# The first block's front of a hybrid conformer/RWKV-7 decoder block: adaLN columns, low parts and the seam to the first projections

## The chip, the cores and the metric

The kernel runs on one core of one Trainium2 chip. The metric is the device time of one execution in microseconds (us); lower is better. The engines are named as the profile names them: PE (TensorE, matmuls), PEld (its weight loads), DVE (VectorE), ACT (ScalarE), POOL (GpSimd) and SP (SyncE, which here issues the DMAs). The engines work side by side, each runs its own instructions in program order, and semaphores hold an instruction until its inputs are there and its output buffer is free. SBUF is the on-chip memory of 128 partitions; PSUM is the memory that PE writes to.

## The reference, cut to what matters

The reference computes one decoder block for a sequence of 2048 tokens and a width of 1024, in float32:

```
mod = silu(c) @ ada_w + ada_b;  shift, scale, gate = split(mod, 3)
h   = rmsnorm(x, norm_g) * (1 + scale) + shift
p   = h @ w_in                       # 73 tiles of 128 columns
...                                  # conv branch and RWKV-7 branch from p
out = (sigmoid(g_conv) * y_conv + sigmoid(g_rwkv) * y_rwkv) @ w_out
x   = rmsnorm(x + gate * out, final_g)
```

The conv branch is a gated causal depthwise convolution with a layer norm. The RWKV-7 branch shifts its inputs by one token (`z + mu * (prev - z)`), has low-rank parts for decay and learning rate (the "LORA" tile of p), and a delta-rule state per head. The change touches only the first lines: `mod` from c, the first h, and the first products with w_in.

## The kernel before, in words

Tokens are worked in four blocks of 512. Activations lie transposed, channels on the 128 partitions, so h of a block is eight tiles of 128 channels by 512 tokens (k = 0 to 7). A float32 product is made of three PE products with the faster type float32r: each operand is split into a high part (a rounding copy on ACT) and a low part (the difference, a subtraction on DVE or POOL), and `mm3k` adds high x high, high x low and low x high. A projection of one weight tile takes 8 x 3 = 24 matmuls of 128x512.

A planner in the kernel's own code orders the later work. `note` (line 116) keeps modelled times for each engine, buffer and DMA; work is written as generators (`Task`, line 215) that yield a function for the time at which they can go on; `poll` (line 223) advances those whose modelled time has come, lower rank first. So the order of the instructions on each engine is fixed when the program is built, and follows from the modelled times up to there. `ahead` (line 629) keeps up to three weight loads (`Load`, line 551) under way: DMA into `w_st`, ACT's copy to `w_hi`, the subtraction to `w_lo`, and stores of both parts for the later blocks. `project` (line 633) takes the next load and a PSUM tile `ps_main` (two buffers, tag "main").

The first block's h is made by `hprep0` (line 813), whose order is written out by hand:

- The row c is loaded to all 128 partitions (`srow`), silu is taken as c * (1 + tanh(c/2)), with the half put in later. Four x tiles of 128 tokens are loaded, the squares of the first two are summed on ACT and of the last two on DVE, and the reciprocal root goes into four scaled identity matrices `dg`.
- `columns(k)` makes two columns of `mod` (shift and scale of channel tile k): two DVE operations over 1024 elements multiply the loaded adaLN rows `ada_st` with `srow` and accumulate. Four such buffers exist; `columns(k)` starts the load of k + 4.
- `turned(k)` transposes and scales x on PE with `dg` into a PSUM tile `ps_x`; ACT adds the columns' scale and shift (`hf`), and `hsplit` (line 784) makes `h_hi` on ACT and `h_lo` on DVE.
- Four weight tiles, in the order LORA, K, R, V, are multiplied with h as h comes: `wsplit` (line 852) splits one, `products(k)` (line 900) catches up with all k before. Their results stay in PSUM as `ps_f`: LORA and K in the two "main" buffers, R and V in two others.
- At k = 4 the loads of the next two weights begin. After the last products both are split, and their further steps become tasks.

After `hprep0` the constants are made on DVE (among them `mu1`, line 1743, which is 1 - mu), and the four tiles are evicted: `lora_split` (line 1540) and `proj` go through `shifted` (line 951), which on ACT makes `t` from PSUM with `mu1`, then two single columns, and on DVE the shifted sum. The first `ps_main` product needs the bank of the LORA tile, and the second that of K.

The weight buffers have tags: "w" has six buffers, which `wr` (line 722) also hands out to loads; "KR" and "tk" have four each and "La" one. A tag's buffers go round in turn, and a new tile waits until the old one's readers are done.

Of the kernel before, what the change touches and what calls it, by code (L numbers as in the profile page):

```python
# [9 lines left out]
F32 = mybir.dt.float32  # L10
F32R = mybir.dt.float32r
# [7 lines left out]
P = 128  # L19
# [24 lines left out]
WB = 6  # L44
LDB = 8
SLACK = 2.0
LEND = 1
LATE_W = ((), (1, 1, 2, 2), (1, 1, 2, 2), (0, 0, 0, 0))
NWX, NRAW, NRAWX, NLD, LDQ, POOLW, PRE = 4, 4, 2, 4, 4.0, 0.0, ()
# [33 lines left out]
def hybrid_block(ctx: ExitStack, tc: tile.TileContext, x, x_t, vecs, convk, w2a2, final_g, ada, w_in, w_co, w_ro, w_o, crow, out,  # L83
# [467 lines left out]
    class Load:  # L551

        def __init__(self, src, task=True):
            self.src, self.here, self.stored, self.hl = src, False, False, None
            self.prior = loads[-2] if len(loads) > 1 else None
            if task:
                Task(self.steps(), 1)

        def steps(self):
            if len(self.src) == 3:  # L560
                yield when(lambda: all(l_.here or len(l_.src) == 3 for l_ in loads))
                yield both(wr.room(1), when(lambda: self.src in wk))
                while len(raws.all) < NRAW:
                    raws.all.extend(slices(wr.take("w_raw").bitcast(F32)))
                    raws.add(*raws.all[-2:])
                    yield wr.room(1)
                yield both(wr.room(1), raws.room())
                raw, t_ = raws.take(), wr.take("w_c")
                slot_ = wr.held.pop(key(t_))
                hi, lo = self.hl = slices(t_)  # L570
                wr.held[key(hi)] = slot_
                nc.sync.dma_start(raw, wk[self.src])
                back = wlow.get(self.src)
                if back is not None:
                    nc.sync.dma_start(lo.bitcast(F32), back.bitcast(F32))
                yield ok(raw)
                nc.scalar.copy(hi, raw)
                if back is None:
                    yield ok(hi)
                    yield some()  # L580
                    quick().tensor_tensor(out=lo, in0=raw, in1=hi.bitcast(F32), op=ALU.subtract)
                raws.give(raw)
                self.here = True
                if back is None and self.src in plan:
                    i_ = "_".join(str(k) for k in self.src)
                    wlow[self.src] = dp.tile([P, TB], F32R, name=f"wl_{i_}", tag=f"wl_{i_}")
                    yield ok(lo)
                    nc.sync.dma_start(wlow[self.src].bitcast(F32), lo.bitcast(F32))
                self.stored = True
                return  # L590
            name, n = self.src
            back = kept.get(self.src)
            if back is not None:
                yield wr.room(2)
                self.hl = wr.take("w_hi"), wr.take("w_lo")
                for t_, b_ in zip(self.hl, back):
                    nc.sync.dma_start(t_.bitcast(F32), b_.bitcast(F32))
                self.here = self.stored = True
                return
            if self.prior is not None:  # L600
                yield when(lambda: self.prior.hl is not None)
            yield wr.room(1)
            st = wr.take("w_st").bitcast(F32)
            nc.sync.dma_start(st, wsrc[name][n])
            yield both(ok(st), wr.room(2))
            hi, lo = self.hl = wr.take("w_hi"), wr.take("w_lo")
            nc.scalar.copy(hi, st)
            yield ok(hi)
            dve = max(now[0], vt["POOL"]) > max(now[0], vt["DVE"]) + W2
            (nc.vector if dve else nc.gpsimd).tensor_tensor(out=lo, in0=st, in1=hi.bitcast(F32), op=ALU.subtract)  # L610
            wr.give(st)
            self.here = True
            if name in KEPT:
                i = "_".join(str(k) for k in (n if isinstance(n, tuple) else (n,)))
                back = [dp.tile([P, KT, P], F32R, name=f"k{p_}_{name}{i}", tag=f"k{p_}_{name}{i}") for p_ in "hl"]
                kept[self.src] = back
                nc.sync.dma_start(back[0].bitcast(F32), hi.bitcast(F32))
                yield ok(lo)
                nc.sync.dma_start(back[1].bitcast(F32), lo.bitcast(F32))
            self.stored = True  # L620
# [40 lines left out]
            nc.sync.dma_start(xt[:, m, :], x[t0:t0 + P, :])  # L661
            xs.append(xt[:, m, :])

    late = ExitStack()
    pm = ctx.enter_context(tc.tile_pool(name="pm", bufs=2, space=PSUM))
    l3 = ctx.enter_context(tc.tile_pool(name="l3", bufs=3))
    c1 = late.enter_context(tc.tile_pool(name="c1", bufs=1))
# [5 lines left out]
    xp = ctx.enter_context(tc.tile_pool(name="xp", bufs=HXB, side="right"))  # L673
    hp = ctx.enter_context(tc.tile_pool(name="hp", bufs=1, side="right"))
    e2 = ctx.enter_context(tc.tile_pool(name="e2", bufs=2, side="right"))
    pa = ctx.enter_context(tc.tile_pool(name="pa", bufs=PAB, space=PSUM))

    ab = vc("ada_b")
    bones = c1.tile([P, P], F32R, name="bones")
# [101 lines left out]
            hx.give(xf)  # L781
        hx.give(row)

    def hsplit(h, k, src):
        hi = hp.tile([P, TB], F32R, name="h_hi", tag="h_hi", bufs=HB)
        lo = hp.tile([P, TB], F32R, name="h_lo", tag="h_lo", bufs=HB)
        with tc.high_priority(HP):
            nc.scalar.copy(hi, src)
            nc.vector.tensor_tensor(out=lo, in0=src, in1=hi.bitcast(F32), op=ALU.subtract)
        h[0].append(hi)  # L790
        h[1].append(lo)

# [18 lines left out]
    front = {}  # L811

    def hprep0():
        srow = l3.tile([P, D], F32, name="srow", tag="KR", bufs=KRB)
        stmp = l3.tile([P, D], F32, name="stmp", tag="KR", bufs=KRB)
        nc.sync.dma_start(srow, crow.unsqueeze(0).broadcast_to([P, D]))
        xs = []
        xload0(xs)
        xload0(xs)
        nc.sync.dma_start(v, vecs)  # L820
        nc.scalar.activation(stmp, srow, AF.Tanh, scale=0.5)
        nc.vector.scalar_tensor_tensor(out=srow, in0=stmp, scalar=1.0, in1=srow, op0=ALU.add, op1=ALU.mult)

        mod = lt.tile([P, 24], F32, name="mod", tag="rn")
        ada_ = []
# [15 lines left out]
        ada_load()  # L841
        wst_load(T_LORA, whl, tag="w", bufs=WB)
        wst_load(T_K, whl, tag="w", bufs=WB)
        ada_load()
        wst_load(T_R, l3, tag="tk", bufs=TKB)
        ada_load()
# [4 lines left out]

        def wsplit():
            i = len(wf_)
            if i < 2:
                hi, lo = [whl.tile([P, KT, P], F32R, name=n_, tag="w", bufs=WB) for n_ in ("w_hi", "w_lo")]
            else:
                hi = l3.tile([P, KT, P], F32R, name="w_f", tag="tk", bufs=TKB)
                lo = (l3.tile([P, KT, P], F32R, name="w_f", tag="tk", bufs=TKB) if i == 2 else
                      lt.tile([P, KT, P], F32R, name="w_f", tag="La", bufs=1))
            nc.scalar.copy(hi, wst[i])  # L860
            nc.vector.tensor_tensor(out=lo, in0=wst[i], in1=hi.bitcast(F32), op=ALU.subtract)
            wf_.append((hi, lo))
            front[tiles_[i]] = (pm, px)[i // 2].tile([P, TB], F32, name="ps_f", tag=("main", "xo")[i // 2])

# [6 lines left out]
        ss = e2.tile([P, 5, NTT], F32, name="ss0", tag="ss0", bufs=1)  # L871
        s2, ss, rs, rt = ss[:, 0:2, :], ss[:, 2, :], ss[:, 3, :], ss[:, 4, :]
        sq_ = [hx0("xsq0") for _ in range(2)]
        for tt in range(NTT // 2):
            for half in range(2):
                hs = slice(half * TB, half * TB + TB)
                nc.scalar.activation(sq_[0], xs[tt][:, hs], AF.Square, accum_out=s2[:, half, tt:tt + 1])
                xd = xs[tt + 2][:, hs]
                nc.vector.scalar_tensor_tensor(out=sq_[1], in0=xd, scalar=1.0, in1=xd, op0=ALU.mult, op1=ALU.mult,
                                               accum_out=s2[:, half, tt + 2:tt + 3])  # L880
        ab, gb = vc("ada_b"), mod[:, 16:24]
        nc.vector.tensor_tensor(out=ss, in0=s2[:, 0, :], in1=s2[:, 1, :], op=ALU.add)
        nc.vector.tensor_scalar(out=ss, in0=ss, scalar1=1.0 / D, scalar2=RMS_EPS, op0=ALU.mult, op1=ALU.add)
# [15 lines left out]

        def products(upto):  # L900
            for i, (w, ti) in enumerate(zip(wf_, tiles_)):
                if i < upto:
                    for kk in range(done_[i], upto):
                        mm3k(front[ti], w, h, kk)
                    done_[i] = upto

        def columns(k):
            for m in range(2):
                nc.vector.scalar_tensor_tensor(out=ada_[k][:, m, :], in0=ada_[k][:, m, :], scalar=0.5, in1=srow,
                                               op0=ALU.mult, op1=ALU.mult, accum_out=mod[:, k + 8 * m:k + 8 * m + 1])  # L910
            if k + 4 < KT:
                ada_load()
# [4 lines left out]
        for k in range(KT):  # L917
# [3 lines left out]
            nc.scalar.activation(shift_col[:, ks], mod[:, ks], AF.Identity, bias=ab[:, ks])  # L921
            nc.scalar.activation(g_col[:, ks], mod[:, gs], AF.Identity, scale=vc("norm_g", k), bias=gb[:, ks])
            if k + 4 == KT:
                for _ in range(2):
                    loads.append(Load(plan.pop(0), False))
                    next_.append(loads[-1].steps())
                    for _ in range(2):
                        next(next_[-1])
                wkeep(0)
                wkeep(1)  # L930
                nc.sync.dma_start(ck, convk)
# [4 lines left out]
            nc.scalar.activation(hf, flat(hp_[k]), AF.Identity, scale=g_col[:, ks], bias=shift_col[:, ks])  # L936
            if k:
                products(k)
            hsplit(h, k, hf)
            if k < 3:  # L940
                wsplit()
        products(KT)
        wkeep(2)
        wkeep(3)
        for steps in next_:
            next(steps)
            w = next(steps)
            Task(steps, 1).when = w
        return h

    def shifted(ps, ti, make):
        mi = ti - T_R
# [776 lines left out]
        yield from pair(G, q, box)  # L1729

    with tc.manual_schedule():
        h = hprep0()
        hlg = cst.tile([P, KT], F32, name="hlg")
        hlb = cst.tile([P, KT], F32, name="hlb")
        nc.vector.tensor_scalar(out=hlg, in0=vc("conv_ln_g"), scalar1=0.5, scalar2=None, op0=ALU.mult)
# [13 lines left out]
        hrk = dcol("hrk", "rwkv_r_k", 0.5, 0.0)  # L1749
        hgg = dcol("hgg", "rwkv_gn_g", 0.5, 0.0)  # L1750
        hgb = dcol("hgb", "rwkv_gn_b", 0.5, 0.0)
        nc.vector.tensor_scalar(out=ck, in0=ck, scalar1=0.5, scalar2=None, op0=ALU.mult)
        side.extend((Task(side_work(), 3), Task(last_norm(), 3)))
        for b in range(NB):
# [538 lines left out]
```

## Time and profile before

| | |
|---|---|
| median of 3 runs | 2684.56 us (2675.53 to 2688.15) |
| profiled execution | 2684.93 us |
| its span, first to last instruction | 2683.2 us |
| mean granted TensorE clock | 0.989 |
| PE busy | 2588.4 us (96%) |
| DVE, POOL, ACT busy | 2186.9, 1316.5, 1189.6 us |
| DMA moved | 712.11 MB, mean 265 GB/s |

A profile row gives the start in us from the first instruction, the duration, the engine, the line, the operation, and out<-in by the program's names; in brackets the idle time of the engine before it and what ended that. Nearly all rows name L194, the helper that records every operation, so tiles tell the rows apart: `ps_x` are the transpositions, `ps_f` the front products, `ps_main` the later projections, `ada_st` the column sums, `xsq` the squares, `mu` is mu1. Matmuls are pipelined, so the distance from start to start counts and not their duration. The granted clock is a share of full speed.

### The profile page before, as it was taken

How to read it: one execution, taken by the hardware profiler on the slowest of the kernel's cores; microseconds unless marked ns; L12 is line 12 of the kernel's file. 1: busy time of each engine (PE TensorE's matmuls, PEld its weight loads, DVE VectorE, ACT ScalarE, POOL GpSimd, SP SyncE). 2: the span in 40 equal slices, each digit the busy share in tenths (PEclk: the TensorE clock that was granted, in tenths of full speed). 3: DMA queues.
4: the chain of work that ended last, by engine and by line, in shares of the span. 5: the costliest groups of instructions: out<-in, count | busy, mean ns of one | idle time of the engine just before them, and what ended most of it. 6: DMA issues, size and time to landing. Idle time of an engine off the chain costs nothing. (4 is left out here: it accounts for less than half of the span.)

```text
span 2683.2 us, 50707 instructions
## 1 busy us (share of the span) xinstructions
PE 2588.4 (96%) x18324; PEld 2083.4 (78%) x18324; DVE 2186.9 (82%) x3663; ACT 1189.6 (44%) x2307; POOL 1316.5 (49%) x1818
## 2 busy tenths in 40 slices
PE   6999999999999999999999999999999998999997
PEld 5877888777877888788778877878887776778786
DVE  6786889788878896978698878888888689898687
ACT  5544444443434433434434333434444454456443
POOL 0576758462558373827583856483727484000000
PEclk9999999999999999999999999999999998999999
DMA  9788778787786688967877888686766778798984
GB/s 351 271 301 309 263 266 284 258 293 232 240 286 237 230 282 270 317 208 269 273 249 237 289 262 263 218 312 207 267 199 213 242 252 300 252 328 313 343 270 161
DMA packets 390835, 712.11 MB, mean 265 GB/s; under 512 B 137508, under 2 KB 141944, under 8 KB 390584
## 3 DMA queue, kind: packets, MB, share of 16 engines
q1 hardware_dynamic: 390584, 708.87, 77.7%
q8 instruction: 144, 2.36, 0.3%
q14 instruction: 107, 0.88, 0.1%
HBM read 494.34 MB, written 213.26 MB: 264 GB/s over the span
## 5 line engine op out<-in xcount | busy, mean ns | idle before, releaser
L194 PE MATMUL ps_main<-h_hi,w_hi 128*128 128x512 f32 x2304 | 923.3, 401 | 7.5 <-DVE lora L194 4.7
L194 PE MATMUL ps_main<-h_hi,w_lo 128*128 128x512 f32 x2304 | 924.8, 401 | 4.4 <-POOL w_lo L194 2.6
L194 PE MATMUL ps_main<-h_lo,w_hi 128*128 128x512 f32 x2304 | 923.0, 401 | 0.0
L194 DVE SCALAR_TENSOR_TENSOR acc<-u,ck,acc 128x512 f32<-128x512 f32 x928 | 698.9, 753 | 26.8
L194 PEld LDWEIGHTS ps_main<-h_hi,w_hi 128*128 128x128 f32 x2304 | 434.8, 189 | 105.9 <-issue 7.6
L194 PEld LDWEIGHTS ps_main<-h_hi,w_lo 128*128 128x128 f32 x2304 | 434.6, 189 | 101.4 <-issue 5.7
L194 PEld LDWEIGHTS ps_main<-h_lo,w_hi 128*128 128x128 f32 x2304 | 435.0, 189 | 93.0 <-issue 5.0
L194 PE MATMUL ps_main<-h_hi,w_c 128*128 128x512 f32 x896 | 291.2, 404 | 6.9 <-DVE mr L194 4.5
L194 POOL TENSOR_TENSOR itmp<-La,TT 128x126 f32<-128x126 f32 (+22 forms) x496 | 204.6, 412 | 46.4 <-issue 13.3
L194 POOL TENSOR_TENSOR TT<-TT,itmp 128x126 f32<-128x126 f32 (+22 forms) x496 | 205.8, 415 | 38.8
L194 ACT ACTIVATE th<-ps_main 128x512 f32<-128x512 f32 x160 | 95.6, 597 | 284.0 <-PE ps_main L194 267.0
L194 PEld LDWEIGHTS ps_main<-h_hi,w_c 128*128 128x128 f32 x896 | 171.6, 192 | 50.3 <-issue 3.9
L194 POOL TENSOR_TENSOR w_lo<-w_st,w_hi 128x1024 fp32r<-128x1024 f32 x55 | 133.4, 2426 | 142.6 <-ACT w_hi L194 131.0
L194 PE MATMUL ps_main<-h_lo,w_c 128*128 128x512 f32 x448 | 180.9, 404 | 13.7 <-DVE h_lo L194 13.6
L194 ACT COPY uv<-xo 64x256 f32<-64x256 f32 (+1 forms) x192 | 80.9, 438 | 210.3 <-PE xo L194 155.1
L194 DVE SCALAR_TENSOR_TENSOR S<-xo,pe,Se 64x64 f32<-64x64 f32 x512 | 123.2, 280 | 49.8 <-PE xo L194 38.5
L194 PE MATMUL ps_main<-w_c,h_hi 128*128 128x512 f32 x448 | 140.1, 393 | 0.0
L194 ACT CAST w_c<-w_raw 128x512 fp32r<-128x512 f32 x168 | 102.1, 619 | 72.0 <-DMA w_raw<-wk_o 27.4
L194 DVE TENSOR_TENSOR As<-aux,maskA 128x512 f32<-128x512 f32 x128 | 82.4, 686 | 47.5 <-PE aux L194 46.9
L194 PEld LDWEIGHTS ps_main<-h_lo,w_c 128*128 128x128 f32 x448 | 86.3, 193 | 35.3 <-DVE h_lo L194 16.0
L194 ACT ACTIVATE Se<-S,pe 128x128 f32<-128x128 f32 x256 | 88.6, 395 | 39.9 <-DVE S L194 38.7
L194 ACT ACTIVATE t<-ps_main,mu 128x512 f32<-128x512 f32 x96 | 65.9, 686 | 80.5 <-PE ps_main L194 80.0
(299 smaller groups left out, 4520.0 us busy)
## 6 DMA issues: line engine op xcount, KB each, us to landing
w_hi<-kh_in SPq DMA_DIRECT2D x219, 512.0 KB
w_lo<-kl_in SPq DMA_DIRECT2D x219, 512.0 KB
w_st<-w_in_t SPq DMA_DIRECT2D x73, 512.0 KB
kh_in<-w_hi SPq DMA_DIRECT2D x71, 512.0 KB
kl_in<-w_lo SPq DMA_DIRECT2D x71, 512.0 KB
lny<-y_d SPq DMA_DIRECT2D x80, 256.0 KB
w_raw<-wk_o SPq DMA_DIRECT2D x56, 256.0 KB
ada_st<-ada_t SPq DMA_DIRECT2D x16, 512.0 KB
```

Source lines behind the costliest of these rows:

```text
L194: r = f(*a, **k)
```

## The change

- silu(c) is computed on one partition (4 KB loaded instead of the row for 128 partitions). Two matmuls with a row of `ones` (which holds 1/1024) spread it into a new PSUM tile `ps_s` of two banks; the columns read it from there, and their factor becomes 0.5 x 1024. That PSUM room is given back before the pool `pa` opens in its place, which therefore opens after the front.
- All eight squares are summed on ACT.
- Low parts: those of weight tiles 0 and 2 stay on DVE (`WDV`), those of 1 and 3 go to POOL; those of h go to POOL, but for k = 7 (`HDV`).
- `products(k)` takes tile i from i <= k instead of i < k.
- The split of weight tile 0 goes into the tag "KR". A "w" buffer is set aside early for the first next weight (`loads[0].st`). At k = 4 both next loads begin as before.
- `hprep0` becomes a generator: it pauses after k = 6, the constants but for the scaling of `ck` are made then, and it goes on with k = 7. Before the last products the first next weight is split; behind them a third load is begun, and only then the parts of tiles 2 and 3 are stored.

```diff
     def hprep0():
-        srow = l3.tile([P, D], F32, name="srow", tag="KR", bufs=KRB)
-        stmp = l3.tile([P, D], F32, name="stmp", tag="KR", bufs=KRB)
-        nc.sync.dma_start(srow, crow.unsqueeze(0).broadcast_to([P, D]))
+        crow_ = lt.tile([P, D], F32, name="crow", tag="La", bufs=1)[0:1]
+        stmp = l3.tile([P, D], F32, name="stmp", tag="KR", bufs=KRB)[0:1]
+        nc.sync.dma_start(crow_, crow.unsqueeze(0))
...
-        nc.scalar.activation(stmp, srow, AF.Tanh, scale=0.5)
-        nc.vector.scalar_tensor_tensor(out=srow, in0=stmp, scalar=1.0, in1=srow, op0=ALU.add, op1=ALU.mult)
+        nc.scalar.activation(stmp, crow_, AF.Tanh, scale=0.5)
+        nc.vector.scalar_tensor_tensor(out=crow_, in0=stmp, scalar=1.0, in1=crow_, op0=ALU.add, op1=ALU.mult)
+        srow = p0.tile([P, 2, TB], F32, name="ps_s", tag="ps_s")
+        for half in range(2):
+            nc.tensor.matmul(srow[:, half], ones[0:1], crow_[:, half * TB:half * TB + TB], start=True, stop=True)
+        srow = flat(srow)
...
         wst_load(T_K, whl, tag="w", bufs=WB)
+        loads.append(Load(plan.pop(0), False))
+        loads[0].st = wr.take("w_st")
...
-            if i < 2:
+            if i == 0:
+                hi, lo = [l3.tile([P, KT, P], F32R, name="w_f", tag="KR", bufs=KRB) for _ in range(2)]
+            elif i == 1:
                 hi, lo = [whl.tile([P, KT, P], F32R, name=n_, tag="w", bufs=WB) for n_ in ("w_hi", "w_lo")]
...
-            nc.vector.tensor_tensor(out=lo, in0=wst[i], in1=hi.bitcast(F32), op=ALU.subtract)
+            (nc.vector if i in WDV else nc.gpsimd).tensor_tensor(out=lo, in0=wst[i], in1=hi.bitcast(F32), op=ALU.subtract)
...
-        for tt in range(NTT // 2):
+        for tt in range(NTT):
             for half in range(2):
                 hs = slice(half * TB, half * TB + TB)
-                nc.scalar.activation(sq_[0], xs[tt][:, hs], AF.Square, accum_out=s2[:, half, tt:tt + 1])
-                xd = xs[tt + 2][:, hs]
-                nc.vector.scalar_tensor_tensor(out=sq_[1], in0=xd, scalar=1.0, in1=xd, op0=ALU.mult, op1=ALU.mult,
-                                               accum_out=s2[:, half, tt + 2:tt + 3])
+                nc.scalar.activation(sq_[half], xs[tt][:, hs], AF.Square, accum_out=s2[:, half, tt:tt + 1])
...
-                if i < upto:
+                if i <= upto:
...
-                nc.vector.scalar_tensor_tensor(out=ada_[k][:, m, :], in0=ada_[k][:, m, :], scalar=0.5, in1=srow,
+                nc.vector.scalar_tensor_tensor(out=ada_[k][:, m, :], in0=ada_[k][:, m, :], scalar=0.5 * D, in1=srow,
...
             if k + 4 == KT:
-                for _ in range(2):
-                    loads.append(Load(plan.pop(0), False))
-                    next_.append(loads[-1].steps())
-                    for _ in range(2):
-                        next(next_[-1])
+                loads.append(Load(plan.pop(0), False))
+                loads[1].prior = None
+                for l_ in loads:
+                    next_.append(l_.steps())
+                    w_ = [next(next_[-1]) for _ in range(2)]
...
-            hsplit(h, k, hf)
+            hsplit(h, k, hf, None if k in HDV else nc.gpsimd)
             if k < 3:
                 wsplit()
+            if k + 2 == KT:
+                yield
+        next(next_[0])
+        first_ = next(next_[0])
         products(KT)
+        ahead()
+        poll()
         wkeep(2)
         wkeep(3)
-        for steps in next_:
-            next(steps)
-            w = next(steps)
+        for steps, w in zip(next_, (first_, w_[1])):
             Task(steps, 1).when = w
-        return h
+        yield h
...
-        h = hprep0()
+        start_ = hprep0()
+        next(start_)
...
         hgb = dcol("hgb", "rwkv_gn_b", 0.5, 0.0)
+        h = next(start_)
+        first.close()
+        pa = ctx.enter_context(tc.tile_pool(name="pa", bufs=PAB, space=PSUM))
         nc.vector.tensor_scalar(out=ck, in0=ck, scalar1=0.5, scalar2=None, op0=ALU.mult)
```

More of the change, by code (lines that the diff above doesn't have):

```diff
@@ L46 @@
 SLACK = 2.0
+WDV = (0, 2)
+HDV = (7,)
 LEND = 1
@@ L553, in __init__ @@
         def __init__(self, src, task=True):
-            self.src, self.here, self.stored, self.hl = src, False, False, None
+            self.src, self.here, self.stored, self.hl, self.st = src, False, False, None, None
             self.prior = loads[-2] if len(loads) > 1 else None
@@ L602, in steps @@
             yield wr.room(1)
-            st = wr.take("w_st").bitcast(F32)
+            st = (self.st or wr.take("w_st")).bitcast(F32)
             nc.sync.dma_start(st, wsrc[name][n])
@@ L662, in xload0 @@
             xs.append(xt[:, m, :])
-    late = ExitStack()
+    late, first = ExitStack(), ExitStack()
     pm = ctx.enter_context(tc.tile_pool(name="pm", bufs=2, space=PSUM))
@@ L675, in hybrid_block @@
     e2 = ctx.enter_context(tc.tile_pool(name="e2", bufs=2, side="right"))
-    pa = ctx.enter_context(tc.tile_pool(name="pa", bufs=PAB, space=PSUM))
+    p0 = first.enter_context(tc.tile_pool(name="p0", bufs=1, space=PSUM))
     ab = vc("ada_b")
@@ L782, in xnorm, with hsplit @@
         hx.give(row)
-    def hsplit(h, k, src):
+    def hsplit(h, k, src, eng=None):
         hi = hp.tile([P, TB], F32R, name="h_hi", tag="h_hi", bufs=HB)
@@ L788, in hsplit @@
             nc.scalar.copy(hi, src)
-            nc.vector.tensor_tensor(out=lo, in0=src, in1=hi.bitcast(F32), op=ALU.subtract)
+            (eng or nc.vector).tensor_tensor(out=lo, in0=src, in1=hi.bitcast(F32), op=ALU.subtract)
         h[0].append(hi)
```

## The prediction

> **What bounds the kernel now.** I read the page's totals first, then the span in stretches of 100 us, then what TensorE (PE) waited for, then the first 60 us instruction by instruction. Page:
>
> ```profile
> span 2683.2 us, 50707 instructions
> PE 2588.4 (96%) x18324; PEld 2083.4 (78%) x18324; DVE 2186.9 (82%) x3663; ACT 1189.6 (44%) x2307; POOL 1316.5 (49%) x1818
> ```
>
> Stretches (columns: length, busy time and count of PE, PEld, DVE, ACT, POOL, granted clock, DMA share, GB/s):
>
> ```profile
> 0.00:100.00 100.00, 77.14 (x365) 62.98 (x366) 73.35 (x142) 52.83 (x99) 25.91 (x26) 0.97 0.88 328
> 100.00:200.00 100.00, 96.58 (x468) 77.12 (x467) 77.16 (x98) 49.91 (x86) 67.68 (x85) 0.98 0.81 286
> 2200.00:2300.00 100.00, 87.61 (x402) 68.02 (x402) 88.68 (x133) 49.06 (x89) 44.20 (x29) 0.93 0.89 303
> 2300.00:2400.00 100.00, 93.35 (x393) 74.67 (x392) 89.09 (x144) 44.00 (x77) 0.00 (x0) 0.97 0.81 278
> ```
>
> PE is the bound. Its 95 us without work sit in the first 100 us (22.9) and about 2200 to 2400 (12.4 and 6.7). The change touches the first 60 us alone; time won there reaches the end only because PE is nearly full behind it. PE's waits over the span (total, times, longest):
>
> ```profile
> PE ps_main L194 <- DVE h_lo L194: 14.9, 6, 5.5
> PE ps_main L194 <- DVE lora L194: 4.7, 1, 4.7
> PE ps_f L194 <- DVE h_lo L194: 3.2, 2, 2.0
> ```
>
> The last two lie in the front. Its end, in order of time (start, duration, engine, what):
>
> ```profile
> 43.09 0.48 PE L194 MATMUL ps_f<-h_hi,w_hi 128*128 128x512 f32 x1
> 49.33 2.00 ACT L194 CAST w_hi<-w_st 128x1024 fp32r<-128x1024 f32 x2 [4.47 <-PE ps_f L194]
> 50.46 2.37 POOL L194 TENSOR_TENSOR w_lo<-w_st,w_hi 128x1024 fp32r<-128x1024 f32 x1 [48.61 <-ACT w_hi L194]
> 51.19 0.40 PE L194 MATMUL ps_f<-h_hi,w_f 128*128 128x512 f32 x1
> 51.36 2.56 DVE L194 TENSOR_TENSOR w_lo<-w_st,w_hi 128x1024 fp32r<-128x1024 f32 x1 [5.78 <-ACT w_hi L194]
> 53.98 0.17 DVE L194 TENSOR_SCALAR mu<-v 128x25 f32<-128x25 f32 x1
> 54.19 0.69 ACT L194 ACTIVATE t<-ps_f,mu 128x512 f32<-128x512 f32 x1 [2.86 <-DVE mu L194]
> 55.44 0.75 DVE L194 SCALAR_TENSOR_TENSOR lora<-ps_f,v,t 128x511 f32<-128x511 f32 x1 [0.52 <-ACT carry L194]
> 56.25 0.80 PE L194 MATMUL ps_main<-h_hi,w_hi 128*128 128x512 f32 x1 [4.66 <-DVE lora L194]
> 59.00 0.26 ACT L194 ACTIVATE carry<-ps_f,v 128x1 f32<-128x1 f32 x1
> 59.68 0.39 PE L194 MATMUL ps_main<-h_hi,w_lo 128*128 128x512 f32 x1
> ```
>
> PE's last front product starts at 51.19; the first of the next projection needs a PSUM bank that the LORA tile holds. That tile was complete at 49.3 (ACT's cast was released then), but its eviction needs mu1, which DVE makes only after the low part of the second next weight. That subtraction ran 2.56 us, because POOL did one at the same time, and mu1 came at 53.98. Then the restart is slow: 56.25 to 59.68 holds 8 starts, 0.43 us each, where 43.09 to 51.19 holds 35 at 0.231. So the seam costs 56.25 - 51.6 = 4.65 us of waiting and 3.43 - 8 x 0.231 = 1.58 us of half clock.
>
> The front before that:
>
> ```profile
> 6.57 0.63 ACT L194 ACTIVATE xsq<-x 128x512 f32<-128x512 f32 x1 [0.30 <-DMA x<-x_in]
> 8.07 0.63 ACT L194 ACTIVATE xsq<-x 128x512 f32<-128x512 f32 x1
> 9.15 0.69 DVE L194 SCALAR_TENSOR_TENSOR xsq<-x 128x512 f32<-128x512 f32 x1 [1.62 <-DMA x<-x_in]
> 11.97 0.08 DVE L194 DVE_READ_ACCUMULATOR xsq<-x 128x1 f32 x1
> 14.49 1.22 DVE L194 SCALAR_TENSOR_TENSOR ada_st<-ada_st,srow 128x1024 f32<-128x1024 f32 x1
> 16.84 1.23 DVE L194 TENSOR_TENSOR w_lo<-w_st,w_hi 128x1024 fp32r<-128x1024 f32 x1
> 16.91 0.38 ACT L194 ACTIVATE g_col<-mod,v 128x1 f32<-128x1 f32 x1
> 18.13 0.62 ACT L194 CAST h_hi<-hf 128x512 fp32r<-128x512 f32 x1
> 18.66 1.04 ACT L194 CAST w_hi<-w_st 128x1024 fp32r<-128x1024 f32 x1
> 39.90 1.22 DVE L194 SCALAR_TENSOR_TENSOR ada_st<-ada_st,srow 128x1024 f32<-128x1024 f32 x1
> 42.28 1.05 PE L194 MATMUL ps_x<-dg,x 128*128 128x128 f32 x8
> ```
>
> DVE runs 16 adaLN column sums (14.49 to 41.12) with the weight and h low parts between them. Stretches of it, and the DMA engines from 5 to 45 us:
>
> ```profile
> 20.00:25.00 5.00, 2.02 (x11) 1.38 (x11) 5.00 (x10) 3.57 (x7) 0.00 (x0) 1.00 1.03 410
> 25.00:30.00 5.00, 4.96 (x19) 4.13 (x20) 5.00 (x7) 3.96 (x7) 0.00 (x0) 0.66 1.03 410
> 5.00:45.00 40.00, 26.80 (x132) 22.76 (x133) 33.41 (x66) 24.94 (x49) 0.00 (x0) 0.96 1.03 411
> ```
>
> DVE is full, PE starves until about 28 us, then runs without a gap to 51.6: late feeding costs PE at the front's end. DMA is full as well, so a quicker DVE soon meets the loads.
>
> **The change part by part.** *Start.* The c row comes as 4 KB for one partition, not 512 KB for 128. ACT and DVE waited for x tiles one and three at 6.57 and 9.15: 1.29 us per 512 KB. All later loads land 1.29 us earlier. Tanh and the product with c take as long on one partition (1024 elements), and two spreading products follow on an idle PE before 14 us: no cost. All eight squares go to ACT: 1.50 us a tile (6.57 to 8.07), from 5.3 to 11.3, against 12.05 on DVE now. The chain behind them starts 0.75 us earlier: column 0 at 13.75, its h_hi at 17.4 to 18.0.
>
> *Columns.* DVE loses two weight low parts (1.14 each, 16.84 to the next start) and seven of h. Now the loads set its pace: twenty transfers of 512 KB follow the last x tile up to the last ada half; 10.45 + 0.2 + 20 x 1.29 = 36.5 now, 35.2 after. With 1.15 us of work behind it the last column ends at 36.4, not 41.1. h(7) is split by 36.4 + 1.9 (g_col start to h_hi end on ACT, 16.91 to 18.75) + 0.7 = 39.0; PE will want it at 44, so 5 us of slack covers DVE, DMA and the eleven small constant operations moved in front of the last step.
>
> *POOL.* The low parts that move cost more there (nanoseconds, least/median/most):
>
> ```profile
> L194 POOL TENSOR_TENSOR w_lo<-w_st,w_hi x55: 2343/2403/2843, 50.5 to 531.3; 128x1024 fp32r<-128x1024 f32 x55
> L194 POOL TENSOR_TENSOR h_lo<-cells,h_hi x15: 1263/1721/1748, 2166.1 to 2237.0; 128x512 fp32r<-128x512 f32 x15
> L194 DVE TENSOR_TENSOR h_lo<-hf,h_hi x40: 628/692/2395, 20.3 to 2147.3; 128x512 fp32r<-128x512 f32 x40
> ```
>
> The columns now read srow from PSUM. That such a DVE operation runs beside POOL unslowed is shown later in the trace, two in 1.29 us:
>
> ```profile
> 93.64 1.28 POOL L194 TENSOR_TENSOR s_lo<-rk,rh 128x512 fp32r<-128x512 f32 x1
> 93.89 1.29 DVE L194 TENSOR_TENSOR As<-aux,maskA 128x512 f32<-128x512 f32 x2 [1.01 <-PE aux L194]
> ```
>
> So I take 1.26 for h and 2.40 for weights; the bounds are 1.75 and 2.84. POOL: h_lo(0) 18.05 to 19.3, K's w_lo to 21.7, h_lo(1) to 23.0. PE starts K's products one k earlier than now, so its queue waits for K's low part (21.7) with the next transposition behind it; harmless, since h(2)'s column ends at 22.1 anyway (nine transfers behind x land at 21.0, and 1.15). From h_lo(1) on PE has work to the end: R's low part on DVE, held by POOL's port until 23.0, ends 24.1 where its products are due at 24.4; V's on POOL ends 27.9, due 28.7. Left are 90 products and four transpositions of 0.81 (42.28 to 43.09): 23.0 + 90 x 0.231 + 4 x 0.81 = 47.0. With POOL at its upper bound h_lo(1) ends at 24.4 and the front at 48.5; POOL's whole load, 7 x 1.75 + 2 x 2.84 = 17.9 us from 18, is still done before PE needs it.
>
> *Cold clock in the front.* Now the 0.66 at 25 to 30 costs PE at most 0.34 x 5 = 1.7 us. PE will again idle some 2.5 us between 18 and 23, less than now. I take half, 0.8 (bounds 0 and 1.7): the front ends at 47.8. The Trainium skill, TensorE: Matmul & The Clock Gate, section "What's actually happening", ties the half clock to an idle window of about 3.4 us; by it no pause here is long enough and the sum would be 0.8 less, but this trace fell to 0.66 behind pauses of at most 2.0 us (the wait for h_lo above), so the measurement decides.
>
> *Seam.* The first next weight gets slots that are free early, is split before the last products, and mu1 is ready. LORA's tile is complete nine products before the end, 45.7; from eviction to restart the trace has 54.19 to 56.25 = 2.06; PE restarts at 47.8 at the earliest, say 48.1, with 0.3 us of pause, too short for a cold clock by any row here. The second weight's split now stands behind LORA's eviction; projection two needs it at 48.1 + 24 x 0.231 = 53.6. If it queues behind all four evictions (54.19 to 59.26, 5.1 us), it ends at 45.7 + 5.1 + 1.04 + 2.4 = 54.2: at most 0.6 us. I take 0. SP holds the third weight's load ahead of four stores; no product waits for these.
>
> *Sum.* Restart 56.25 - 48.1 = 8.15 earlier, and 1.58 of half clock gone: 9.7 us. Bounds: all of POOL's and the clock's upper ends and 0.6 for the second weight give 9.7 - 1.5 - 0.9 - 0.6 = 6.7; the lower end of the clock gives 10.5. The profiled execution took 2684.93 (1.7 us around its span), the median of the runs is 2684.56: 2684.9 - 9.7 = 2675.
>
> **The rivals.** *The gain is not carried.* All later order is written from modelled times that shift here. If 2000 us of rearranged work give the 9.7 back, the time is 2684. Against it: PE at 96 to 100% in nearly all later stretches. For it: some 53 us of small waits (95 - 22.9 - 19) that a new order can move.
>
> *The change of stages gets shorter.* From 2200 to 2400 PE lacks 19 us, 8 of them in waits for h_lo, and runs at 0.93 and 0.97. If the new order halves the waits for h_lo and part of the slow clock with them, 8 us more go: 2667.
>
> *It gets longer, and the kernel slower.* Same place, other sign: half as much again of those 19 us (9.5) and 5 us of cold clock make 14.5, so 2690. It decides from 9.7 us on. The 5.5 us wait shows that one operation out of place there costs that much.
>
> *POOL binds the front.* Bounds above: 2678; it lies in the forecast's own range.
>
> **How the numbers follow.** Forecast 2675, own range 2671 to 2680: 0.57. Not carried, 2684: 0.15. Shorter change of stages, 2667: 0.18. Longer, 2690: 0.10. About 0.5% (13.4 us) is what a measurement of this kernel can tell from no change: faster than 2671 is nearly all of the 2667 case and a tail of the forecast, 0.22; over 2698 is the far part of the 2690 case, 0.06; the rest, 0.72, is within. The range 2665 to 2688 leaves out the ends of the 2667 and 2690 cases.
>
> **What would show it.** Right: h low parts on POOL at 1.3 us; the last column near 36.4; the last front product near 47; mu1 before 40; the first ps_main product near 48 with no wait for lora over 1 us and starts 0.23 apart; all later marks 9 to 10 us earlier. Wrong: DVE columns stretched beside POOL; a new PE wait for w_lo at 53; a cold clock after 48; or the front won and the stretch 2200 to 2400 changed by more than 5 us.

## The result, and the profile after

The changed kernel takes 2673.56 us in the median of 12 runs (2668.82 to 2679.79); 12 runs of the kernel before beside it take 2683.43 (2672.99 to 2694.58). The ratio is 0.9964 with a 95% interval of 0.9952 to 0.9977, so the kernel is 9.9 us faster, 0.36%; 9.7 us were forecast. That is a real gain and a small one, inside the half per cent that the prediction called "within".

The profiled execution of the changed kernel took 2679.79 us, the slowest of its 12, and so its span is only 5.3 us shorter than before's. Single executions of after lie up to 11 us apart here, those of before up to 22. The gain is therefore read from medians, and the place where it arises from the first 60 us of the traces. The page's totals:

```profile
span 2677.9 us, 50719 instructions
PE 2591.1 (97%) x18328; PEld 2082.4 (78%) x18328; DVE 2177.5 (81%) x3645; ACT 1191.8 (45%) x2315; POOL 1330.8 (50%) x1828
```

The same four stretches of 100 us as before, with the same columns:

```profile
0.00:100.00 100.00, 87.25 (x414) 69.23 (x415) 70.25 (x132) 61.17 (x120) 46.06 (x41) 1.00 0.93 349
100.00:200.00 100.00, 96.53 (x471) 77.20 (x471) 80.79 (x101) 48.06 (x80) 73.11 (x96) 1.00 0.84 297
2200.00:2300.00 100.00, 87.36 (x376) 67.58 (x375) 88.17 (x133) 48.27 (x86) 38.49 (x26) 0.93 0.88 300
2300.00:2400.00 100.00, 93.35 (x393) 74.83 (x393) 89.61 (x146) 44.71 (x80) 0.00 (x0) 0.97 0.83 283
```

Of these four only the first changed: PE is busy for 87.25 us of it instead of 77.14. The two stretches at the change of stages, of which two rivals expected 8 us less or 14.5 more, have the same PE time to 0.3 us and the same granted clock. PE's waits over the span (total, times, longest):

```profile
PE ps_main L196 <- DVE h_lo L196: 15.0, 6, 5.6
PE ps_main L196 <- POOL w_lo L196: 3.8, 4, 1.7
PE ps_f L196 <- POOL w_lo L196: 1.1, 1, 1.1
```

The waits for `lora` (4.7) and for the front's `h_lo` (3.2) are gone. The first row is the change of stages, as before. The front itself, rows picked from the timeline in order of start:

```profile
13.25 1.21 DVE L196 SCALAR_TENSOR_TENSOR ada_st<-ada_st,ps_s 128x1024 f32<-128x1024 f32 x1
...
18.83 2.37 POOL L196 TENSOR_TENSOR w_lo<-w_st,w_hi 128x1024 fp32r<-128x1024 f32 x1
18.92 0.50 PE L196 MATMUL ps_f<-h_lo,w_f 128*128 128x512 f32 x1 [0.48 <-POOL h_lo L196]
19.95 1.22 DVE L196 SCALAR_TENSOR_TENSOR ada_st<-ada_st,ps_s 128x1024 f32<-128x1024 f32 x1 [0.84 <-DMA ada_st<-ada_t]
21.16 1.28 POOL L196 TENSOR_TENSOR h_lo<-hf,h_hi 128x512 fp32r<-128x512 f32 x1
21.25 0.50 PE L196 MATMUL ps_f<-h_hi,w_lo 128*128 128x512 f32 x1 [1.14 <-POOL w_lo L196]
22.40 0.48 PE L196 MATMUL ps_f<-h_hi,w_f 128*128 128x512 f32 x1
35.69 1.22 DVE L196 SCALAR_TENSOR_TENSOR ada_st<-ada_st,ps_s 128x1024 f32<-128x1024 f32 x1
37.91 0.17 DVE L196 TENSOR_SCALAR mu<-v 128x25 f32<-128x25 f32 x1
41.30 2.41 POOL L196 TENSOR_TENSOR w_lo<-w_st,w_hi 128x1024 fp32r<-128x1024 f32 x1 [3.40 <-ACT w_hi L196]
44.90 0.69 ACT L196 ACTIVATE t<-ps_f,mu 128x512 f32<-128x512 f32 x1 [3.73 <-PE ps_f L196]
46.53 0.39 PE L196 MATMUL ps_f<-h_hi,w_f 128*128 128x512 f32 x1
47.04 0.51 PE L196 MATMUL ps_main<-h_hi,w_hi 128*128 128x512 f32 x1
47.39 0.40 PE L196 MATMUL ps_main<-h_lo,w_hi 128*128 128x512 f32 x1
```

A column that runs beside POOL (19.95) takes 1.22 us as the first one does. After 22.40 PE has no gap: the last front product starts at 46.53 and the first `ps_main` product 0.51 later. `mu1` is made at 37.91, seven microseconds ahead of the eviction that needs it (44.90). In stretches of 5 us the clock stays full where before had 0.66 (25 to 30):

```profile
20.00:25.00 5.00, 3.86 (x21) 3.27 (x21) 4.75 (x7) 4.54 (x8) 3.02 (x3) 1.00 1.03 410
25.00:30.00 5.00, 5.00 (x27) 4.25 (x26) 4.70 (x9) 3.55 (x8) 4.39 (x3) 1.00 1.03 410
```

One wait is new, and no step of the prediction had it: that for the low part of the third next weight.

```profile
53.49 0.41 ACT L196 CAST wl<-wf 128x256 fp32r<-128x256 f32 x1 [1.42 <-DMA wf<-w2a]
54.92 0.63 ACT L196 ACTIVATE xt<-xt 128x512 f32<-128x512 f32 x1 [0.53 <-DMA xt<-x_in]
56.16 1.03 ACT L196 CAST w_hi<-w_st 128x1024 fp32r<-128x1024 f32 x1
57.33 2.38 POOL L196 TENSOR_TENSOR w_lo<-w_st,w_hi 128x1024 fp32r<-128x1024 f32 x1 [2.36 <-ACT w_hi L196]
59.76 0.51 PE L196 MATMUL ps_main<-h_hi,w_lo 128*128 128x512 f32 x1 [0.98 <-POOL w_lo L196]
```

ACT takes that weight at 56.16, behind two operations that waited for DMAs. PE's products start at 58.39 and then only at 59.76, 1.14 us later than their pitch. So at 60 us the change stands at 9.21 (restart 56.25 to 47.04) + 1.58 (half clock gone) - 1.14 = 9.65 us, and the medians show 9.9 at the end. The 9.21 carries the spread of single executions: in another one of the same kernel (e11) the front starts 0.7 us earlier and the restart comes at 46.36.

A later mark shows how the lead goes on in this execution, the slowest of its 12. These are the DMA issues of `dA` in before and after (least, median and longest in ns, then the start of the first and the last in us):

```profile
L194 SPq DMA_DIRECT2D dA<-As x128: 302/449/1627, 137.4 to 2082.1; - x128
L196 SPq DMA_DIRECT2D dA<-As x128: 302/449/1779, 128.0 to 2077.7; - x128
```

The first is 9.4 us earlier, the last only 4.4. The prediction's sign that all later marks come 9 to 10 us earlier is thus seen up to 137 us; behind that it is borne out by the medians and not by this trace.

### The profile page after: what moved, and what is told of

Read it like the earlier page. It is cut to its first block, busy times and chain, and to the rows that moved or that the text cites. A ratio compares the mean times of both kernels' runs of the same rounds, so it can differ in the third digit from the quotient of the medians.

```text
span 2677.9 us, 50719 instructions
## 1 busy us (share of the span) xinstructions
PE 2591.1 (97%) x18328; PEld 2082.4 (78%) x18328; DVE 2177.5 (81%) x3645; ACT 1191.8 (45%) x2315; POOL 1330.8 (50%) x1828
## 5 line engine op out<-in xcount | busy, mean ns | idle before, releaser
L196 PE MATMUL ps_main<-h_lo,w_c 128*128 128x512 f32 x448 | 180.5, 403 | 13.8 <-DVE h_lo L196 13.7
```

Source lines behind the costliest of these rows:

```text
L196: r = f(*a, **k)
```

## The experiments

For each kernel the table gives two marks, counted from its own first transposition of x (the first `ps_x` start), because that start itself lies anywhere from 12.8 to 13.8 us in kernels with the same code up to there (13.81 in after, 13.10 in e11); of before there is one trace, with 15.05. Times with an interval are medians of 6 or 12 executions against the kernel before on the same chip; "1 run" is one execution.

| kernel | last front product | first `ps_main` | time, us | ratio to before |
|---|---|---|---|---|
| before | 36.14 | 41.20 | 2683.4 | |
| after | 32.72 | 33.23 | 2673.6 | 0.9964 (0.9952 to 0.9977) |
| e1, new front, old seam | 32.74 | 37.88 | 2680.0 | 0.9991 (0.9978 to 1.0004) |
| e2, old front, new seam | 35.71 | 36.14 | 2676.9 | 0.9974 (0.9964 to 0.9985) |
| e3, 80 more products | 32.73 | 51.27 | 2695.3 | 1.0050 (1.0033 to 1.0067) |
| e4, planner + 2 us | 32.74 | 33.25 | 2673.7 | 0.9962 (0.9945 to 0.9979) |
| e5, constants late | 32.72 | 33.23 | 2676.9, 1 run | |
| e6, h low parts on DVE | 36.14 | 36.57 | 2682.5, 1 run | |
| e7, products from i < k | 33.64 | 34.15 | 2676.8, 1 run | |
| e8, srow in SBUF | 37.34 | 37.85 | 2693.4, 1 run | |
| e9, later stores | 32.74 | 33.25 | 2677.4 | 0.9980 (0.9966 to 0.9995) |
| e10, planner + 6 us | 32.74 | 33.25 | 2682.8 | 1.0001 (0.9987 to 1.0014) |
| e11, after once more | 32.75 | 33.26 | 2674.9 | 0.9967 (0.9951 to 0.9982) |

**e1: the new front with the old seam.** Low parts, squares, silu and products as after; the next two weights are split behind the last products with the old buffers, and the constants come after all of it.

```diff
...
-        next(next_[0])
-        first_ = next(next_[0])
         products(KT)
-        ahead()
-        poll()
         wkeep(2)
         wkeep(3)
-        for steps, w in zip(next_, (first_, w_[1])):
+        for steps in next_:
+            next(steps)
+            w = next(steps)
             Task(steps, 1).when = w
...
```

> The changed kernel with the seam as before (weight tile 0 and the next weights in the old buffers, both next weights split behind the last products, constants made after that). Theory (the gain is made in the first 57 us and carried one for one): last front product near 46.5 as in the changed kernel, pause of about 4.7 us and a stretch at half clock as before, first ps_main product near 51.5, total about 6 us over the changed kernel, 2679 to 2680. Rival (the order of the later work gives the gain): the total need not follow the restart, and may be at 2674 or at 2684.

Its timeline, end of the front:

```profile
45.91 2.56 DVE L196 TENSOR_TENSOR w_lo<-w_st,w_hi 128x1024 fp32r<-128x1024 f32 x1 [5.76 <-ACT w_hi L196]
48.53 0.17 DVE L196 TENSOR_SCALAR mu<-v 128x25 f32<-128x25 f32 x1
50.87 0.80 PE L196 MATMUL ps_main<-h_hi,w_hi 128*128 128x512 f32 x1 [4.75 <-DVE lora L196]
51.47 0.63 PE L196 MATMUL ps_main<-h_lo,w_hi 128*128 128x512 f32 x1
```

The stall is back as it was: DVE's 2.56 us subtraction, `mu1` behind it, PE's wait of 4.75 us, and then products 0.43 us apart until 55.73. The front keeps its gain: from first transposition to last front product it takes 32.74 us (after 32.72, before 36.14). The time is 2680.0 against 2683.4, but its interval (0.9978 to 1.0004) includes no change, so these 3.4 us are not clear of noise.

**e2: the old front with the new seam.** All low parts on DVE, two x tiles' squares on DVE, products from i < k. Silu stays on one partition and in PSUM.

```diff
-WDV = (0, 2)
-HDV = (7,)
+WDV = (0, 1, 2, 3)
+HDV = tuple(range(8))
...
-                if i <= upto:
+                if i < upto:
```

> The changed kernel with all low parts of the front on DVE, products from i < k and the squares shared by ACT and DVE as before; silu stays in PSUM, the seam stays new. Theory: last front product at 50 to 51, pause under 0.5 us, no half clock behind it, first ps_main product near 51, total about 4 us over the changed kernel, 2677 to 2678. Rival: the total does not follow the restart.

The pause at the seam is 0.20 us beyond the pitch (49.09 to 49.52), and products follow 0.23 apart. The time is 6.5 us under before. With 3.4 from e1 that makes 9.9, the whole change, but that it fits so well is luck: both kernels keep the earlier start, which is thus counted twice. The marks leave the start out. By them the restart is 3.3 us earlier in e1, 5.1 in e2 and 8.0 in after, so front and seam add up to within 0.4 us; with the 1.58 of half clock, which e2 does not have, the seam is about two thirds. The trace held a surprise in the front, part of why the restart came at 49.52 where 51 was expected: first PE's timeline and then the stretches of 5 us:

```profile
23.36 0.50 PE L196 MATMUL ps_f<-h_lo,w_f 128*128 128x512 f32 x1 [2.01 <-DVE h_lo L196]
```

```profile
20.00:25.00 5.00, 2.99 (x17) 2.43 (x17) 5.00 (x8) 4.00 (x7) 0.00 (x0) 1.00 1.03 411
25.00:30.00 5.00, 4.21 (x23) 3.37 (x22) 5.00 (x9) 2.92 (x6) 0.00 (x0) 1.00 1.02 408
```

The same pause of 2.01 us that stood ahead of before's 0.66 left the clock at 1.00 here.

**e3: is time at the seam carried to the end?** Eighty more products between the front and the seam, past the planner, so that the order of all later work stays. They write the PSUM tile of silu(c), which nobody reads any more; their result is not used.

```diff
         products(KT)
+        for _ in range(80):
+            tc.nc.tensor.matmul(srow[:, 0:TB], wf_[0][0][:, 0, :], h[0][0], start=True, stop=True)
         ahead()
```

> The changed kernel with 80 extra matmuls of 128x512 on PE behind the last front products, written past the planner, so that every later instruction keeps its place; their result is not used. Theory: the restart comes 80 x 0.23 = 18.4 us later (near 65.4), the wait for the third weight (1.1 us) goes, and the total rises by 17 us, to about 2691: a us at the seam is a us at the end. Rival (the later stages absorb what happens at the start): a rise under 9 us.

The restart moved 18.0 us (33.23 to 51.27), the wait for the third weight is gone, and the median lies 21.7 above after's. So all of it is carried. The intervals reach 4.6 us to either side here and 3.4 in after, so the 3.7 us beyond what was put in are not clear of noise.

**e4 and e10: what the planner's order is worth.** The planner's modelled time is put forward by 2 and by 6 us behind the front. No work changes, only the order of what follows.

```diff
+        now[0] += 2.0        # 6.0 in e10
         side.extend((Task(side_work(), 3)
```

> The changed kernel with the planner's modelled PE time put 2.0 us ahead once, behind the front: the front is untouched, and the later order is another one. Theory: the total stays within 3 us of 2673.6. Rival (order alone is worth as much as the gain): it moves by 5 us or more.

> The changed kernel with the planner's modelled PE time put 6.0 us ahead once behind the front: a third order of the later work with the same front. Theory: within 4 us of the changed kernel, 2670 to 2678. Rival (order alone is worth as much as the gain): it moves by 5 us or more.

With 2 us the time did not move (2673.7). The wait for the third weight fell to 0.23 us there, because ACT took it at 54.68 ahead of the x tile's operations; a wait of 1.18 us for `lw` came behind it. With 6 us the front and the restart are after's, and yet the time is 2682.8, 8 us above e11 on the same chip. My theory expected 2670 to 2678 and fell. SP's one load of a weight between 27.3 and 57.3 us, ACT and PE behind the restart, and the clock in stretches of 20 us:

```profile
42.97 0.33 SPq L196 DMA_DIRECT2D w_st<-w_in_t  x1
47.10 1.05 ACT L196 CAST w_hi<-w_st 128x1024 fp32r<-128x1024 f32 x1 [1.74 <-DMA w_st<-w_in_t]
57.11 1.03 ACT L196 CAST w_hi<-w_st 128x1024 fp32r<-128x1024 f32 x1
58.20 0.79 PE L196 MATMUL ps_main<-h_hi,w_hi 128*128 128x512 f32 x1 [6.14 <-ACT w_hi L196]
58.79 0.63 PE L196 MATMUL ps_main<-h_lo,w_hi 128*128 128x512 f32 x1
60.68 0.80 PE L196 MATMUL ps_main<-h_hi,w_lo 128*128 128x512 f32 x1 [1.26 <-POOL w_lo L196]
```

```profile
40.00:60.00 20.00, 13.15 (x53) 9.63 (x52) 4.99 (x8) 11.33 (x26) 8.00 (x5) 0.90 0.96 353
60.00:80.00 20.00, 19.32 (x71) 15.34 (x72) 11.08 (x15) 9.51 (x17) 5.91 (x7) 0.84 0.58 220
```

PE waits after 24 products, so it wants the second weight, and gets it from the copy at 57.11. The copy at 47.10 waited for a load, and SP issued those of the first two weights from 26.38 on and then only the one at 42.97, which is the third weight's; so the third weight went ahead while the second lay ready. That reading is inferred from the counts and from SP's order, since rows do not name the weight. The sum is plain: 6.14 + 1.26 of waiting against e11's 1.34, and some 15 products at 0.43 instead of 0.23, make 9 us at 70 us. One copy out of place in an unchanged amount of work has cost by there nearly as much as the whole change won. That the loss reaches the end rests on the medians, whose intervals do not overlap: the two profiled executions end at 2679.9 and 2679.4, e11's being the slowest of its 12. Other effects of the new order further on are not excluded.

**e5: the constants' place.** They are made after the last products again, all else as after.

```diff
         next(start_)
+        h = next(start_)
         hlg =
...
-        h = next(start_)
         first.close()
```

> The changed kernel with the constants (mu1 among them) made behind the whole front instead of ahead of its last step. Theory (what was in mu1's way was the second next weight's low part on DVE, and that now comes later): DVE is idle from 40.9 on, the constants take 0.9 us there, and LORA's eviction starts unchanged when its products end, about 31.1 us behind the first transposition; restart unchanged within 0.2 us. Rival (the constants' place is what shortens the seam): restart a us or more later.

The restart is the same to 0.01 us. DVE's timeline:

```profile
40.22 0.17 DVE L196 TENSOR_SCALAR mu<-v 128x25 f32<-128x25 f32 x1
...
40.60 2.40 DVE L196 TENSOR_SCALAR ka<-v 128x8 f32<-128x8 f32 x1
```

`mu1` comes at 40.22, since no low part of a weight stands ahead of it on DVE any more. So this part of the change was not needed. The second row is a trap beside it: eight elements took 2.40 us, to 43.00, while POOL's `w_lo` ran from 40.52 to 42.97.

**e6: the low parts of h back on DVE.** The weight parts stay as after.

```diff
-HDV = (7,)
+HDV = tuple(range(8))
```

> The changed kernel with all of h's low parts on DVE. Theory: DVE's work for one k (2.3 for the columns and 0.6) is now longer than the loads need (2.58), each low part stands behind the next two columns, and the last column ends at 38 to 40; PE's backlog hides nearly all of it: restart 0 to 1 us later than in the changed kernel, from first transposition to restart 33.2 to 34.2 us. Rival (POOL for h is what feeds PE in time): 2 us or more later.

The restart is 3.34 us later, not 0 to 1, and the last front product stands at 36.14, as before: all of the front's gain is lost. Timeline of the place:

```profile
17.70 2.36 POOL L196 TENSOR_TENSOR w_lo<-w_st,w_hi 128x1024 fp32r<-128x1024 f32 x1 [15.85 <-ACT w_hi L196]
18.19 2.42 DVE L196 TENSOR_TENSOR h_lo<-hf,h_hi 128x512 fp32r<-128x512 f32 x1
20.66 0.51 PE L196 MATMUL ps_f<-h_lo,w_f 128*128 128x512 f32 x1 [1.98 <-DVE h_lo L196]
```

DVE's subtraction of two SBUF tiles is held until POOL's ends and takes 2.42 us instead of 0.69, PE waits 1.98, and behind that the clock falls, in the stretches of 5 us:

```profile
20.00:25.00 5.00, 4.34 (x16) 3.86 (x17) 5.00 (x8) 3.41 (x7) 0.06 (x1) 0.67 1.02 407
```

So POOL is not only relief for DVE's load: it is what keeps h's low parts out of the turn-taking with the weight's.

**e7: products from i < k.**

```diff
-                if i <= upto:
+                if i < upto:
```

> The changed kernel with products from tiles i < k as before. Theory: three products fewer are done before h's second tile is split, so three more stand in the gapless part: restart 0.7 us later, from first transposition to restart 33.9 us. Rival (the earlier start of K only makes PE wait for K's low part): restart unchanged or earlier.

The restart is 0.92 us later. That is what the one word is worth.

**e8: silu(c) copied to SBUF.** The columns read it there and no longer in PSUM.

```diff
-        srow = flat(srow)
+        srow_ = l3.tile([P, D], F32, name="srow_", tag="BK", bufs=BKB)
+        nc.scalar.copy(srow_, flat(srow))
+        srow = srow_
```

> The changed kernel with the spread silu row copied from PSUM to SBUF (one ACT copy of about 1 us near 9 us) and the columns reading it there. Theory (DVE with two SBUF inputs and POOL hold each other up): columns that meet a POOL operation take up to 3.6 us instead of 1.2, or POOL's operations up to 2.4 and 3.6 us instead of 1.3 and 2.4, the last column ends at 40 or later, and the restart comes 1 to 5 us later. Rival (where the row lies does not matter): column and POOL durations and restart unchanged.

Timeline of DVE and POOL where they meet:

```profile
21.80 1.50 POOL L196 TENSOR_TENSOR h_lo<-hf,h_hi 128x512 fp32r<-128x512 f32 x1 [19.94 <-ACT h_hi L196]
22.09 2.28 DVE L196 SCALAR_TENSOR_TENSOR ada_st<-ada_st,srow__457 128x1024 f32<-128x1024 f32 x1
23.25 3.33 POOL L196 TENSOR_TENSOR w_lo<-w_st,w_hi 128x1024 fp32r<-128x1024 f32 x1
24.30 3.37 DVE L196 SCALAR_TENSOR_TENSOR ada_st<-ada_st,srow__457 128x1024 f32<-128x1024 f32 x1
26.55 2.25 POOL L196 TENSOR_TENSOR h_lo<-hf,h_hi 128x512 fp32r<-128x512 f32 x1
```

The two engines now take turns. The column at 24.30 is long because it waits until POOL's `w_lo` ends at 26.58 and then needs its 1.1 us; POOL's next subtraction in turn waits for it. From its first transposition the restart is 4.6 us later than after's. (That first transposition is itself 4.2 us late: the copy waits on ACT for PE's spreading products, with the squares behind it.) The one run of 2693.4 lies 19.9 us above after's median; the restart, 8.8 us later in all (47.04 to 55.86), accounts for less than half of that, and the rest is open.

**e9: the stores behind the seam put off.** The stores of the split parts of tiles 2 and 3 become tasks 12 and 24 us later, to let ACT's inputs through earlier.

```diff
-        wkeep(2)
-        wkeep(3)
+        def keep_later():
+            for i in (2, 3):
+                yield after(12.0)
+                wkeep(i)
+
+        Task(keep_later(), 1)
```

> The changed kernel with the four stores of the split R and V tiles put off by 12 and 24 us of planner time, so that the loads behind them on SP's queue (low-rank weights, the next x) are issued earlier. Theory (the third weight's cast on ACT stands behind operations that wait for these loads): the wait of PE for the third weight's low part (1.1 us at 59.8) goes, at most 1 us of the total, which the timing cannot tell from nothing: 2671 to 2675. Rival (the third weight is late for its own load or slots): the wait stays.

The wait for the third weight is 0.58 us instead of 1.34 in e11: shorter, but not gone as the theory expected. The time is 2677.4 against 2674.9, and the intervals overlap, so no gain is seen.

**e11: the changed kernel again**, on the chip of e9 and e10.

> The changed kernel itself, on the chip of the two runs beside it, as their base. All theories: 2673 to 2676, and the marks of its front as in its first profile.

It took 2674.9, and its front's marks are after's.

## Why the prediction was right, point by point

**Start.** The first column was to move from 14.49 to 13.75, and it came at 13.25. That is a late one: in the nine other traces with the same start (all but e2 and e8) it comes at 12.24 to 12.55. This step was mis-sized, by 0.5 to 1.5 us: ACT's squares began at 4.78 (4.63 to 4.93 in the others), while 1.29 before 6.57 would be 5.28. No run takes the start away alone, and there is one trace of before, so its worth is not known better than that.

**Columns.** The last one ends at 36.91; 36.4 was forecast. The loads do set the pace: the columns at 19.95 and others now wait for `ada_st`.

**POOL.** The lower prices held (1.28 for h, 2.37 to 2.41 for weights), and `h_lo(1)` was ready at 22.44 instead of 23.0. The bet that a column which reads PSUM is not slowed by POOL rested on one pair of rows; e8 shows what it was worth, 4.6 us. The Trainium skill, SBUF — State Buffer, section "Who interferes with whom", states this rule: a DVE instruction with at most one SBUF input, outside the faster two-port modes, does not contend with GpSimd, and one with two SBUF inputs does. After (1.22) and e8 (2.28 and 3.37) agree with it.

**Cold clock in the front.** I took half of 1.7 us as left, and there was none. PE's pauses were 0.48 and 1.14 us, where 2.5 in all were forecast. This step was mis-sized by 0.8; it is most of why PE restarted at 47.04 and not at 48.1, and the earlier start is the rest. By the window of about 3.4 us that the Trainium skill, TensorE: Matmul & The Clock Gate, section "What's actually happening", gives, there was to be none, and after agrees; e6 does not, with 0.67 around a pause of 1.98. Nor does PE starve until about 28 us in before, as I wrote: its last pause in the front ends at 25.05, and from there to 28.40 products run 0.43 apart.

**Seam.** A pause of 0.3 was forecast, and the start-to-start distance of 0.51 leaves that over the pitch of 0.231. No half clock follows. The cause that I gave, `mu1` behind DVE's low part of the second weight, is what e1 brings back. But I listed three things together: an early split, free buffers and early constants. e5 shows that the constants' place is worth nothing once the low part has left DVE. The early split and the free buffers were not taken apart.

**What the prediction missed.** "I take 0" was right for the second weight, whose low part was ready at 50.66 for 52.7. It did not go one weight further: the third is split behind ACT operations that wait for DMAs, and costs 1.14 us. I followed SP's order only as far as the stores, and not to the loads behind them that ACT's queue waits for. So the sum of 9.7 came out this close by luck: a restart 1.06 us better than forecast paid for a wait of 1.14 that the forecast lacked.

**The rivals.** *Not carried* fell: e3's later restart came out in full at the end, and the medians of the change agree with the front's sum. *POOL binds* fell by its rows. *The change of stages shorter* or *longer* fell in these traces, with equal PE time there. The fear behind them, that the order written from modelled times can cost as much as the edit wins, was sound, but I looked for it 2100 us too late: e10 shows it 6 us behind the seam.

## What to carry to other kernels

When a small operation stands on the path, look at what is queued ahead of it on its own engine: here 0.17 us of constants cost 4.65 us of PE and a cold clock. Before work is given to POOL, ask what DVE does beside it: an operation with one input in PSUM went on at full speed, while two SBUF inputs made the engines take turns. When a wait is removed, follow each queue to the next two or three deliveries, not only to the first, because the next late one takes its place.

## What the runs showed of the hardware

- The length of one pause did not decide whether the clock fell. Behind a pause of 2.01 us before had 0.66 over 5 us and e2 had 1.00; e6 had 0.67 around a pause of 1.98. What PE did ahead of the pause, or when it fell, may count; no run here separates these.
- A DVE operation of eight elements per partition (`ka` in e5, otherwise 0.16 us) took 2.40 us beside POOL's subtraction, with a single tensor input. I had looked for this only in large operations.
- Operations that contend are not slowed in proportion. In e8 each waited for the other to end, so that a column of 1.22 us took 2.28 or 3.37, by what POOL had under way.
